# An eight-core trunk kernel: pooling mixer moved into the previous FFN, norm squares summed on GpSimd, first loads reordered

## The chip, the cores and the metric

The kernel runs on one Trainium2 chip, as one program on all eight cores. Each core works on one of the eight sequences of the batch, and the cores do not exchange data. The metric is device time in microseconds (us) of the slowest core, and lower is better.

Engine names are as in the profile: PE is the matrix engine (PEld its weight loads), DVE the vector engine, ACT the scalar engine, POOL GpSimd, SP the engine that issues most DMAs. Cores 0 to 3 form die 0, cores 4 to 7 die 1.

Executions of one kernel fall into two states. In the fast state all cores show nearly the same granted TensorE clock (0.969 to 0.987 of full speed, as a mean over the execution) and times mostly agree within about 0.3%. In the slow state the cores of one die, or of both, show a lower clock and the time is longer. Only fast runs are compared below. A second number is given beside them: the slowest core of each die that was undisturbed (all four clocks at 0.9715 or more), averaged over such dies, even where the other die was slow. It is called "undisturbed dies". It sits a few us under the fast runs, since it takes the slowest of four cores instead of eight, and that core's own span.

## The reference, cut to what matters

```python
D_MODEL = 1024; BATCH = 8; SEQ = 4096; DEPTH = 4; D_FF = 2816
POOL_WINDOWS = (2, 4, 8, 16)      # trailing windows of four channel groups of 256

def reference(x, c, ...):
    c_act = silu(c)
    for i in range(DEPTH):
        mod = c_act @ ada_w[i] + ada_b[i]
        sh1, sc1, g1, sh2, sc2, g2 = split(mod, 6)
        h = rmsnorm(x, norm_mix_g[i]) * (1.0 + sc1) + sh1
        # i % 3: 0 short gated conv, 1 conformer conv, 2 multi-scale pool
        y = mixer(h)
        x = x + g1 * y
        h = rmsnorm(x, norm_ffn_g[i]) * (1.0 + sc2) + sh2
        x = x + g2 * swiglu(h, ffn_w_in[i], ffn_w_out[i])
    return rmsnorm(x, final_g)

def multiscale_pool(h, w_grp, scale):
    # per group g: mean over the last w_g tokens minus the token, then a 256x256 linear
    ...
```

Layers 0 and 3 use the short convolution ("M" below), layer 1 the conformer convolution ("B"), layer 2 the pool ("C"). Every layer ends in a SwiGLU FFN ("F").

## The kernel before

A core holds its sequence channel-major: 8 chunks of 128 channels by the tokens. It goes through the sequence in four blocks of 1024 tokens, s0 to s3. The work of one part of a layer on one block is a *stage* (F1 s3 is the FFN of layer 1 on the last block). A stage is a list of *units*, a unit being one weight slab; each unit is emitted for both halves of the block (`nt` = 0 and 1, 512 tokens each, the width of one projection matmul, 128x512 in the profile). Between the half-units of the current stage the kernel emits small tasks of other work, above all the norm of the next stage; the positions are called *slots* here, and `spread(tasks, lo, hi)` distributes tasks over slots. In the timelines below each engine takes its instructions in the order in which they were emitted (behind the matmuls at 3128.68 us, below, PE stood for 25.45 us before a ones-matmul, with matmuls of the same pool unit emitted behind it).

A norm needs the sum of squares over all 1024 channels, which run along partitions. ACT squares a chunk and PE multiplies it with a matrix of ones, which adds over the partitions and accumulates over the chunks:

```python
def stats_chunk(xk, c, nt):
    bk, bkb = statbank(nt)
    k = sqctr[nt] % 2
    ...
    P.op("act", lambda e: e.activation(sqr2[:, nt, k, :], xres[:, xk, c, tsl(nt)], AF.Square), ...)

    def mm():
        P.op("pe", lambda e: e.matmul(bk, ones_bf[:, :], sqr2[:, nt, k, :], start=(c == 0), stop=(c == 7)), ...)

    pend_stats[nt].append(mm)

def rstd_make(nt):
    flush_stats(nt)                     # emits the pending ones-matmuls
    bk, bkb = statbank(nt)
    rsqrt_eps(rstd_t[:, nt, :], bk, [bkb], [rstdb[nt]])   # two ACT instructions
```

So one norm of a block is 8 chunks times 2 halves, 16 ones-matmuls.

For the pool, the same task that normalises a chunk also forms its window sums on DVE: log2(window) shifted adds (`for l in range(1, g + 2)`), one to four of them:

```python
def norm_pool(xk, c, nt, gs, sh, deps, hk, s):
    tk = norm_chunk(xk, c, nt, gs, deps)          # DVE
    g = c // 2
    w = 2 << g
    H, Hb = scr()
    P.op("act", lambda e: e.activation(H[:, 15:527], tmp_t[:, tk, :], AF.Identity, ...))
    ...                                            # two small DVE copies of 15 columns
    for l in range(1, g + 2):
        ...
        P.op("dve", lambda e: e.tensor_tensor(Sx[:, a:527], prev[:, a:527], prev[:, a - sh_:527 - sh_], ALU.add), ...)
    P.op("dve", lambda e: e.scalar_tensor_tensor(hbuf[...], prev[:, 15:527], 1.0 / w, H[:, 15:527], ALU.mult, ALU.subtract), ...)
```

The pool mixer was the first unit of its own stage "CF"; its norm for the FFN was a second unit without any matmul of its own:

```python
def units_C(st):
    def emit(nt, u):
        slab, slabb = get_slab(u, nt)
        for c in range(8):
            bk, bkb = bank()                       # one of six PSUM banks in rotation
            ...                                    # 2 matmuls
            resid(st, bk, bkb, c, nt, ..., mode="stats")   # DVE: x += ..., then stats_chunk
    unit(st, emit, ("M", 0))

    def emit_norm(nt, u):
        rstd_make(nt)
        for c in range(8):
            norm_h(xk, c, nt, ...)
    unit(st, emit_norm)
...
def ahead(st, part, i, s, frac=None):              # the next stage's norm, inside this stage
    a, b = 2 * st["first"], 2 * st["end"] - 3
    steps = pre_steps(sts[(part, i, s)])
    ...
    spread(steps[:2], t0, t0 + 2)                  # loads
    spread(steps[2:12], t1, t2)                    # squares, ones-matmuls, rstd
    spread(steps[12:], t2, b + 1)                  # norm (and window sums)
```

Weights arrive in f32. The slabs of the first mixer are cast to bf16 by the DMA that loads them, and written back for the later blocks; all other slabs are converted in DRAM beforehand (`conv_tasks`, f32 read and bf16 written), those of the first FFN during stages M0. The slab ring in SBUF has four places. At the start, the ring's loads were issued first:

```python
issue_loads()                                      # four cast loads of weights
st0 = sts[("M", 0, 0)]
pre0 = pre_steps(st0)
pre0[0]()                                          # x of the first half
for t in range(22):
    ada_dma(0, t, ...)                             # conditioning weights
pre0[1]()                                          # x of the second half
...
```

Of the kernel before, what the change touches and what calls it, by code (L numbers as in the profile page):

```python
# [16 lines left out]
F = 2816  # L17
# [243 lines left out]
def build():  # L261
# [14 lines left out]
    with es:  # L276
# [73 lines left out]

        ctr = dict(nb=6, us=0, bank=0, tmp=0, sg=0, scr=0, ub=0)

# [72 lines left out]

        seq = []
        wstate = dict(loaded=0, used=0, done=0)

        def load_slab(g):
# [3 lines left out]
            if s == 0 and (i, p) == (0, "M"):  # L433
                P.op("pool", lambda e: e.dma_start(out=wring[:, k, 0:L], in_=wsrc(i, p, q)), writes=[wb[k]], sem=f"wc{k}", inc=16)
                P.op("sp", lambda e: e.dma_start(out=wdst(i, p, q), in_=wring[:, k, 0:L]), reads=[wb[k]],
                     writes=[wdb[(i, p, q)]], sem=f"wr{k}", inc=16)
            elif s == 0 and name == "bconv":
# [20 lines left out]
        def next_slab():  # L458
            g = wstate["used"]
            assert wstate["loaded"] > g, ("slab not loadable", g, wstate)  # L460
            wstate["used"] += 1
            k = g % NRING
            return wring[:, k, :], wb[k]

# [80 lines left out]
        def rsqrt_eps(out, src, reads, writes):  # L545
            P.op("act", lambda e: e.activation(out, src, AF.Ln, bias=small[:, 16:17], scale=1.0), reads=reads + [constb], writes=writes)  # L546
            P.op("act", lambda e: e.activation(out, out, AF.Exp, bias=small[:, 17:18], scale=-0.5), reads=writes + [constb], writes=writes)  # L547

        def rstd_make(nt):
# [86 lines left out]
        def resid(st, bk, bkb, c, nt, gvec, deps, bias=None, mode="store"):  # L636
# [13 lines left out]
            if mode == "store":  # L650
                x_store(xk, s, nt, c)
            else:
                stats_chunk(xk, c, nt)
# [234 lines left out]
        def units_C(st):  # L888
            i, s, hk, xk = st["i"], st["s"], st["hk"], st["xk"]
# [4 lines that stand above are left out]
                    g, m = c // 2, c % 2  # L894
                    bk, bkb = bank()

                    def fn(pe):
                        for kc in range(2):
                            o = (g * 2 + kc) * 256 + m * 128
                            ins = pe.matmul(bk, slab[:, o:o + 128], hbuf[:, hk, 2 * g + kc, tsl(nt)], start=(kc == 0), stop=(kc == 1))  # L900
                        return ins

                    P.op("pe", fn, reads=[slabb, hb[hk][2 * g][nt], hb[hk][2 * g + 1][nt]], writes=[bkb])
                    resid(st, bk, bkb, c, nt, der[:, i, 16 + c:17 + c], [derb[i][2]], mode="stats")
            unit(st, emit, ("M", 0))

            def emit_norm(nt, u):
                rstd_make(nt)
                for c in range(8):
                    norm_h(xk, c, nt, der[:, i, 8:16], modT[:, i, 24:32], [derb[i][1], modb[i][3]], hk)  # L910
            unit(st, emit_norm)

        def units_F(st, inner=None):
            i, s, hk, xk = st["i"], st["s"], st["hk"], st["xk"]
# [34 lines left out]
            for c in range(8):  # L949
                mk_out(c)  # L950
            if last:
                def emit_out(nt, u):
# [5 lines left out]

        def pre_steps(st):
            part, i, s, xk, hk = st["part"], st["i"], st["s"], st["xk"], st["hk"]  # L960
# [10 lines left out]

            def sq(nt, c):
                flush_stats(nt)
                stats_chunk(xk, c, nt)
                stats_chunk(xk, c + 1, nt)

            def hh(nt, c):
                if part == "CF":
                    norm_pool(xk, c, nt, gs, sh, deps, hk, s)
# [5 lines left out]
            for nt in range(2):  # L985
                for c in range(0, 8, 2):
                    steps.append(lambda nt=nt, c=c: sq(nt, c))
                steps.append(lambda nt=nt: rstd_make(nt))
            for nt in range(2):
# [23 lines left out]

        def ahead(st, part, i, s, frac=None):
            a, b = 2 * st["first"], 2 * st["end"] - 3
            if part is None:
                return
            steps = pre_steps(sts[(part, i, s)])
            if st["part"] == "M":
                t0, t1, t2 = a + 2, a + (b - a) * 3 // 10, a + (b - a) * 6 // 10  # L1020
            else:
                t0, t1, t2 = a + 2, a + 6, a + 22
            if st["part"] == "F" and st["i"] == 3:
                b -= 2
            spread(steps[:2], t0, t0 + 2)
            spread(steps[2:12], t1, t2)
            spread(steps[12:], t2, b + 1)

# [20 lines left out]
        sts[("B3", 1, 3)] = st3  # L1049

        def inner_b3():
            st3["first"] = len(units)
# [3 lines left out]
        for s in range(NPAIR):  # L1056
            stage("F", 1, s, s % 2, lambda st: units_F(st, inner_b3 if s == 0 else None))
        for s in range(NPAIR):
            def cf(st):
                units_C(st)  # L1060
                units_F(st)
            stage("CF", 2, s, s % 2, cf)
        for s in range(NPAIR):
# [7 lines left out]
        for s in range(NPAIR):  # L1071
# [4 lines left out]
            mid = lo + (hi - lo) // 2  # L1076
            spread(steps[2:12], lo - 3, mid)
            spread(steps[12:], mid, hi + 1)
            x3 = pre_steps(sts[("B3", 1, s)])
# [4 lines left out]
            else:  # L1084
# [6 lines left out]
        spread(steps[:2], a, a + 2)  # L1091
        spread(steps[2:12], a + 4, a + 14)
        spread(steps[12:], a + 14, b + 1)
        chain = ([("F", 1, s) for s in range(1, NPAIR)] + [("CF", 2, s) for s in range(NPAIR)]
                 + [("M", 3, s) for s in range(NPAIR)] + [("F", 3, s) for s in range(NPAIR)])
# [8 lines left out]
        for i in range(3):  # L1104
            lo, hi = span("CF" if i == 2 else "F", i, 0, 3)
            spread(ada_tasks(i + 1, range(96)), lo + 4, hi - 12)
# [14 lines left out]
        spread(conv_tasks([(2, "M"), (2, "F")]), lo, hi - 20)  # L1121
        lo, hi = span("CF", 2)
        spread(conv_tasks([(3, "M")]), lo, hi - 20)
        lo, hi = span("M", 3)
        spread(conv_tasks([(3, "F")]), lo - 60, hi - 20)


        issue_loads()
        st0 = sts[("M", 0, 0)]
        pre0 = pre_steps(st0)  # L1130
        pre0[0]()
        for t in range(22):
            ada_dma(0, t, hid2[:, t * 1024:(t + 1) * 1024].bitcast(F32), [hidb[t][0], hidb[t][1]], f"ah{t}", q="sp")
        pre0[1]()
        for fn in pre0[2:12]:
            fn()
        for t in range(22):
            ada_mul(0, t, hid2[:, t * 1024:(t + 1) * 1024].bitcast(F32), [hidb[t][0], hidb[t][1]])
        for fn in ada_tasks(0, range(22, 32)):
            fn()  # L1140
        P.op("dve", lambda e: e.tensor_scalar(der[:, 1, 24:32], vcol("bb1", 8, 8), 0.5, None, ALU.mult), reads=[vecsb], writes=[derb[1][3]])
        P.op("pool", lambda e: e.dma_start(out=wtab[:, :, :, :].rearrange("p a b c -> p (a b c)"), in_=convw_d[:, :]), writes=[wtabb], sem="cvw", inc=16)
# [5 lines left out]
        P.op("sp", lambda e: e.dma_start(out=bones_f[:, :], in_=convc_d[:, 32:160]), writes=[bonesb], sem="cvf", inc=16)  # L1148
        for fn in pre0[12:]:
            fn()  # L1150

# [63 lines left out]
```

## Time and profile before

| | before |
|---|---|
| time, three runs | 5703.26 us median (5702.33 to 6167.07; the last one is slow) |
| profiled core | core 5, 5694.1 us |
| PE busy | 5264.6 us, 92% |
| first projection begins | 93.8 us |
| ones-matmuls | 36 norms x 16 = 576 |
| stretch of the pool layer, F1 s3 to the start of M3 | 1357.0 us |

These are lines of the profile page of the kernel before: the span, the busy time of each engine, and three groups of instructions. A group's columns are source line, engine, operation, output and inputs with their shapes, count, then busy us and mean ns of one, then the engine's idle time just before these instructions and what ended most of it.

```profile
span 5694.1 us, 73906 instructions; the slowest of 8 cores (5674.9 to 5694.1 us)
PE 5264.6 (92%) x24528; PEld 2412.1 (42%) x24528; DVE 2461.0 (43%) x4314; ACT 1620.5 (28%) x2507; POOL 558.4 (10%) x916
...
L627 PE MATMUL psum<-hbuf,wring 128*128 128x512 bf16 x15872 | 3500.6, 381 | 80.1 <-ACT hbuf L563 24.1
...
L540 PE MATMUL psum<-sqr,ones_bf 128*128 128x512 bf16 x576 | 201.6, 400 | 277.4 <-ACT sqr L537 272.1
...
L813 POOL TENSOR_TENSOR hid<-hid 128x512 f32<-128x512 f32 x60 | 99.6, 1660 | 410.0 <-DVE hid L797 409.5
```

PE is busy for 92% of the span, so it is the engine to look at. Its real work is the two projection groups at L627. The ones-matmuls at L540 are 576 of some 24,500 matmuls, yet PE stood idle before them for 277 us: they are where PE waits. POOL does little compute; L813 shows an add of its costing 1.66 us.

Where PE waits is told by windows, which give the busy time of every engine in chosen stretches of time. Columns: start and end of the window, its length, then busy us and count for PE, PEld, DVE, ACT and POOL, the granted clock, the DMA share and GB/s. I take a stage to begin at the first weight load of its projection. The lines are of the kernel before: from the start to the first projection, the four blocks of M0, and the stretch from F1 s3 to the start of M3, which holds all four pool blocks with their FFNs and one plain FFN stage.

```profile
0.00:93.80 93.80, 8.81 (x16) 1.67 (x16) 29.84 (x83) 21.20 (x32) 11.10 (x24) 1.00 0.84 222
93.80:611.10 517.30, 470.70 (x2079) 205.46 (x2080) 352.43 (x713) 130.78 (x214) 77.46 (x144) 0.96 0.79 199
...
2897.10:4254.10 1357.00, 1219.52 (x5553) 544.50 (x5552) 583.90 (x1083) 387.88 (x581) 106.87 (x199) 0.96 0.42 130
```

At full clock one of these matmuls takes 0.2158 us from start to start (1072 matmuls in 231.4 us of a plain FFN stage). The pool stretch has 5552 weight loads, one per matmul, and 5552 x 0.2158 = 1198 us. The PE's waits in the pool layer's stretch of the kernel before (what PE waited for, us in total, times, longest):

```profile
PE psum L540 <- ACT sqr L537: 127.5, 41, 25.5
PE psum L627 <- ACT hbuf L563: 9.7, 4, 2.4
```

The view says "ACT's squares". The timeline of the kernel before, at one of these stops, shows that ACT is only the last link. Columns: start, duration, engine, line, operation; in brackets idle time and what ended it.

```profile
3128.68 1.03 PE L900 MATMUL psum<-hbuf,wring 128*128 128x512 bf16 x4
...
3134.84 0.74 DVE L642 SCALAR_TENSOR_TENSOR xres<-psum,modT,xres 128x512 f32<-128x512 f32 x1
3135.50 0.74 DVE L556 SCALAR_TENSOR_TENSOR tmp<-xres,der,rstd 128x512 f32<-128x512 f32 x1
...
3137.52 2.29 DVE L590 TENSOR_TENSOR aux<-aux 128x518 f32<-128x518 f32 x3
3139.91 0.69 DVE L593 SCALAR_TENSOR_TENSOR hbuf<-aux 128x512 bf16<-128x512 f32 x1
...
3153.55 1.40 DVE L642 SCALAR_TENSOR_TENSOR xres<-psum,der,xres 128x512 f32<-128x512 f32 x2
...
3155.16 0.58 PE L540 MATMUL psum<-sqr,ones_bf 128*128 128x512 bf16 x1 [25.45 <-ACT sqr L537]
```

At 3128.68 PE does the first four matmuls of a pool unit. The ones-matmul emitted behind them needs the square of the first pool residual. That residual (L642 with `der`, at 3153.55) stands on DVE behind window sums of further chunks (L556, L590 with three adds in the lines shown, L593), each of which keeps DVE for 5 to 6 us, and behind residuals of the previous FFN (L642 with `modT`). PE gets to go on at 3155.16, after 25.45 us. DVE works nearly all the while; it only waits some 0.9 us in each chunk for the ACT step of the same window sum.

### The profile page before, as it was taken

What the parts mean: (1) busy time and instruction counts of PE and PEld (TensorE: products, weight loads), DVE (VectorE), ACT (ScalarE), POOL (GpSimd) and SP (SyncE); (2) the same over time, 40 slices, a digit from 0 to 9 for tenths busy, and PEclk for the clock granted to TensorE, in tenths of its full rate; (3) what the DMA queues carried; (4) which work ended last, traced back from release to release, by engine and by line L of the source; (5) the groups of instructions that cost most, each with busy time, mean ns of one, the idle gap of its engine ahead of it and who ended that gap; (6) DMA issues with size and microseconds to landing.
All of it is one profiled execution on the core that took longest, in us unless ns stands there. A gap on an engine that the chain in (4) does not pass through costs nothing.

```text
span 5694.1 us, 73906 instructions; the slowest of 8 cores (5674.9 to 5694.1 us)
## 1 busy us (share of the span) xinstructions
PE 5264.6 (92%) x24528; PEld 2412.1 (42%) x24528; DVE 2461.0 (43%) x4314; ACT 1620.5 (28%) x2507; POOL 558.4 (10%) x916
## 2 busy tenths in 40 slices
PE   3889999999988888999999797979899999999998
PEld 1334444444444444444444343434344444444443
DVE  4667432332285655333224454545326663223222
ACT  2222222122234443222212323232312322323221
POOL 1111110110022111111000010101000000000000
PEclk9999999999998999999999899989999999999999
DMA  7888576854345655666442344435445543233132
GB/s 194 220 212 207 167 177 174 212 146 150 114 168 191 209 204 193 187 191 180 147 153 97 120 137 135 138 132 143 133 130 174 158 138 134 93 112 137 66 111 75
DMA packets 252179, 876.86 MB, mean 154 GB/s; under 512 B 29072, under 2 KB 62096, under 8 KB 220944
## 3 DMA queue, kind: packets, MB, share of 16 engines
q1 hardware_dynamic: 185808, 583.39, 30.9%
q0 software_dynamic: 66000, 288.75, 20.2%
q8 instruction: 205, 3.36, 0.2%
q14 instruction: 166, 1.36, 0.1%
HBM read 813.12 MB, written 219.68 MB: 181 GB/s over the span
## 4 chain that ended last, share of the span: by engine, by line
PE 81%; DVE 7%; DMA 5%; ACT 3%; issue 3%; SPq 0%; DVEq 0%; POOL 0%; ACTq 0%; POOLq 0%
PE psum L627 78%; PE psum L540 2%; DMA xres<-xT 2%; DVE tmp L556 1%; PE psum L790 1%; DMA wring<-wbf 1%; DVE aux L590 1%; DMA wring<-wpack 1%; ACT sqr L537 1%; DMA aux<-adaw 1%; ACT hbuf L563 1%; DVE xres L642 1%; DVE tmp L848 0%; DVE tmp L846 0%; ACT L546 0%
## 5 line engine op out<-in xcount | busy, mean ns | idle before, releaser
L627 PE MATMUL psum<-hbuf,wring 128*128 128x512 bf16 x15872 | 3500.6, 381 | 80.1 <-ACT hbuf L563 24.1
L627 PEld LDWEIGHTS psum<-hbuf,wring 128*128 128x128 bf16 x15872 | 1557.1, 98 | 1977.5 <-issue 138.4
L627 PE MATMUL psum<-hid,wring 128*128 128x512 bf16 x6656 | 1456.3, 379 | 8.4 <-DVE hid L695 8.4
L934 DVE TENSOR_TENSOR hid<-psum,sg 128x512 bf16<-128x512 f32 x704 | 485.1, 691 | 1772.0 <-PE psum L627 1507.3
L627 PEld LDWEIGHTS psum<-hid,wring 128*128 128x128 bf16 x6656 | 650.7, 98 | 794.8 <-issue 12.1
L933 ACT ACTIVATE sg<-psum 128x512 f32<-128x512 f32 x704 | 417.9, 596 | 1506.4 <-PE psum L627 1470.2
L642 DVE SCALAR_TENSOR_TENSOR xres<-psum,modT,xres 128x512 f32<-128x512 f32 x384 | 281.4, 748 | 628.2 <-PE psum L627 624.1
L563 ACT ACTIVATE hbuf<-tmp,modT 128x512 bf16<-128x512 f32 x448 | 313.9, 722 | 800.1 <-DVE tmp L556 799.2
L537 ACT ACTIVATE sqr<-xres 128x512 bf16<-128x512 f32 x576 | 337.3, 622 | 587.5 <-DVE xres L642 332.6
L540 PE MATMUL psum<-sqr,ones_bf 128*128 128x512 bf16 x576 | 201.6, 400 | 277.4 <-ACT sqr L537 272.1
L556 DVE SCALAR_TENSOR_TENSOR tmp<-xres,der,rstd 128x512 f32<-128x512 f32 x512 | 388.9, 788 | 16.3 <-ACT rstd L547 16.3
L618 POOL DMA_DIRECT2D xd<-xres x384 | 209.1, 545 | 1640.4 <-DVE xres L642 876.9
L468 POOL DMA_DIRECT2D aux<-adaw x362 | 195.5, 541 | 1342.3 <-DVE aux L473 1120.2
L473 DVE SCALAR_TENSOR_TENSOR aux<-aux,cbc 128x512 f32<-128x512 f32 x362 | 247.3, 683 | 116.9 <-DMA aux<-adaw 115.0
L540 PEld LDWEIGHTS psum<-sqr,ones_bf 128*128 128x128 bf16 x576 | 57.0, 99 | 392.7 <-issue 348.5
L790 PE MATMUL psum<-aux,wring 128*128 128x256 bf16 x1152 | 160.3, 292 | 37.5 <-DMA wring<-wbf 17.4
L685 ACT ACTIVATE sg<-psum 128x512 f32<-128x512 f32 x128 | 75.6, 591 | 380.0 <-PE psum L627 350.2
L686 DVE TENSOR_TENSOR aux<-psum,sg 128x512 f32<-128x512 f32 x128 | 88.6, 692 | 193.1 <-ACT sg L685 184.5
L790 PEld LDWEIGHTS psum<-aux,wring 128*128 128x128 bf16 x1152 | 118.2, 104 | 70.9 <-issue 43.8
L813 POOL TENSOR_TENSOR hid<-hid 128x512 f32<-128x512 f32 x60 | 99.6, 1660 | 410.0 <-DVE hid L797 409.5
L577 ACT ACTIVATE aux<-tmp,modT 128x512 f32<-128x512 f32 x64 | 46.2, 722 | 301.7 <-DVE tmp L556 301.7
L422 POOL DMA_DIRECT2D wbf<-wpack x93 | 47.6, 512 | 764.1 <-PE psum L627 413.4
(72 smaller groups left out, 1679.0 us busy)
## 6 DMA issues: line engine op xcount, KB each, us to landing
wring<-wbf SPq DMA_DIRECT2D x214, 1024.0 KB, 5.8
xres<-xd SPq DMA_DIRECT2D x112, 1024.0 KB, 11.4
xd<-xres POOLq DMA_DIRECT2D x384, 256.0 KB, 3.6
aux<-adaw POOLq DMA_DIRECT2D x362, 256.0 KB, 5.2
wring<-wbf SPq DMA_DIRECT2D x128, 704.0 KB, 4.3
wbf<-wpack POOLq DMA_DIRECT2D x52, 1024.0 KB, 13.1
wring<-wbf SPq DMA_DIRECT2D x56, 768.0 KB, 6.1
wring<-wbf SPq DMA_DIRECT2D x48, 576.0 KB, 5.5
```

The source lines that it names most:

```text
L468: P.op(q, lambda e: e.dma_start(out=dst, in_=adaw[i, eh]), writes=bufs, sem=sem, inc=16)
L473: P.op("dve", lambda e: e.scalar_tensor_tensor(src, src, 1.0, cbc[:, hf * 512:(hf + 1) * 512], ALU.mult, ALU.mult, accum_out=raw[:, eh:eh ...
L537: P.op("act", lambda e: e.activation(sqr2[:, nt, k, :], xres[:, xk, c, tsl(nt)], AF.Square), reads=[xb[xk][c][nt]], writes=[sq2b[nt][k]])
L540: P.op("pe", lambda e: e.matmul(bk, ones_bf[:, :], sqr2[:, nt, k, :], start=(c == 0), stop=(c == 7)), reads=[sq2b[nt][k], constb], writes= ...
L556: P.op("dve", lambda e: e.scalar_tensor_tensor(tmp_t[:, tk, :], xres[:, xk, c, tsl(nt)], gs[:, c:c + 1], rstd_t[:, nt, :], ALU.mult, ALU.m ...
L563: P.op("act", lambda e: e.activation(hbuf[:, hk, c, tsl(nt)], tmp_t[:, tk, :], AF.Identity, bias=sh[:, c:c + 1], scale=1.0), reads=[tmpb[t ...
L618: P.op("pool", lambda e: e.dma_start(out=xd[s, nt, c], in_=xres[:, xk, c, tsl(nt)]), reads=[xb[xk][c][nt]], writes=[xdb[s][nt][c]], sem=f" ...
L627: ins = pe.matmul(bk, slab[:, k * stride + col0:k * stride + col0 + 128], rhs_fn(k, nt), start=(k == 0), stop=(k == kchunks - 1))
L642: P.op("dve", lambda e: e.scalar_tensor_tensor(xs, bk, gvec, xs, ALU.mult, ALU.add), reads=[bkb] + deps, writes=[xb[xk][c][nt]])
L790: ins = pe.matmul(bk[:, 0:256], slab[:, par * CW + d * 128:par * CW + (d + 1) * 128], uP[:, g, 8 - d:264 - d], start=(d == 0), stop=(d == ...
L933: P.op("act", lambda e: e.activation(sg_t[:, k, :], gt, AF.Silu), reads=[gtb], writes=[sgb[k]])
L934: P.op("dve", lambda e: e.tensor_tensor(hid(hp(f), nt), up, sg_t[:, k, :], ALU.mult), reads=[upb, sgb[k]], writes=[hidb[hp(f)][nt]])
```

## The change

The change has three parts.

1. *Pool mixer in the previous FFN.* The pool unit of block s+1 is placed inside the FFN of block s, behind its third output unit (of block 0, inside F1 s3). Its window sums fall into the slots before; its FFN norm into the slots behind it. The stage "CF" is gone.
2. *Norm squares summed on GpSimd.* ACT squares into f32, POOL adds the eight squares of a half block, and PE does one ones-matmul per half instead of eight. This is done for 23 of the 36 norms, those without it being the norms prepared inside a short-convolution stage, the first one and the final one. It takes 322 matmuls away and puts 322 adds on POOL. With it the slots of the norms move: squares now end two slots earlier, and both halves' rstd are made in one task.
3. *First loads in the order of need.* The conditioning weights and x of the first half are issued first, the four cast loads of weights wait for them (`gate`), and x of the second half is used later. The write-back of the first slabs is issued when a slab is used, not when it is loaded.

```diff
         def load_slab(g):
             if s == 0 and (i, p) == (0, "M"):
-                P.op("pool", lambda e: e.dma_start(out=wring[:, k, 0:L], in_=wsrc(i, p, q)), writes=[wb[k]], sem=f"wc{k}", inc=16)
-                P.op("sp", lambda e: e.dma_start(out=wdst(i, p, q), in_=wring[:, k, 0:L]), ...)
+                P.op("pool", lambda e: e.dma_start(out=wring[:, k, 0:L], in_=wsrc(i, p, q)), writes=[wb[k]],
+                     after=[gate[g]] if g in gate else [], sem=f"wc{k}", inc=16)
...                                      (the write-back moves to next_slab)
+        def sumsq_chunk(xk, c, nt):
+            src = xres[:, xk, c, tsl(nt)]
+            if c == 0:
+                P.op("act", lambda e: e.activation(rstd_t[:, nt, :], src, AF.Square), ...)
+                return
+            k = nxt("sf", 2)
+            ...
+            P.op("act", lambda e: e.activation(sq, src, AF.Square), reads=[xb[xk][c][nt]], writes=sq2b[k])
+            if c < 7:
+                P.op("pool", lambda e: e.tensor_tensor(rstd_t[:, nt, :], rstd_t[:, nt, :], sq, ALU.add), ...)
+                return
+            tot = rstd_t[:, nt, 0:256].bitcast(BF16)
+            P.op("pool", lambda e: e.tensor_tensor(tot, rstd_t[:, nt, :], sq, ALU.add), ...)
+            def mm():
+                P.op("pe", lambda e: e.matmul(bk, ones_bf[:, :], tot, start=True, stop=True), ...)
...
         def units_C(st):
-                    resid(st, bk, bkb, c, nt, ..., mode="stats")
+                    resid(st, bk, bkb, c, nt, ..., mode="keep")
-            def emit_norm(nt, u):  ...
-        def units_F(st, inner=None):
+        def units_F(st, inner=None, late=None):
             for c in range(8):
                 mk_out(c)
+                if c == 2 and late is not None:
+                    late()
...
         def ahead(...):
+            if (part, i) == ("F", 2):
+                c = sts[("C", 2, s)]
+                pool = pre_steps(c)
+                n = 2 * c["first"]
+                spread(pool[:2], a, a + 2)              # loads
+                spread(pool[2:10], a + 3, a + 6)        # squares
+                spread(pool[10:], a + 8, n - 2)         # norm and window sums
+                spread(steps[2:10], n + 1, n + 4)       # squares of the FFN norm
+                spread(steps[10:], n + 6, b + 1)        # FFN norm
+                return
             spread(steps[:2], t0, t0 + 2)
-            spread(steps[2:12], t1, t2)
-            spread(steps[12:], t2, b + 1)
+            spread(steps[2:10], t1, t2 - 2)
+            spread(steps[10:], t2, b + 1)
...
+        for n in range(4):
+            ada_quad(n)                                 # conditioning weights
+        pre0[0]()                                       # x, first half
+        landed = [ada_quad(n) for n in range(4, 8)]
+        gate.update({0: landed[0], 1: landed[2], 2: landed[3], 3: landed[3]})
         issue_loads()
-        pre0[0]()  ...
```

## The prediction

Two passages are cut from the text, where it is marked. No term of its sum is among them: 180 + 30 + 15 + 15 = 240 us stands as it was recorded.

> **What bounds the kernel now.** The TensorE: the page gives PE 92% of 5694 us, the chain of waits puts 78% on projection matmuls. A plain FFN stage runs 231.4 us for 1056 + 16 matmuls (timeline), 0.216 us each, clock 1.00: time is won only by removing matmuls or closing gaps. Gaps (windows, PE waits): 94 us before the first projection; about 45 us in each of four conformer blocks; and the pool layer's stretch, 2965 to 4345 us. Its 5408 projection and pool matmuls need 1167 us, its ones-matmuls 31, yet it takes 1380: 182 us of gaps and of slow matmuls behind them (clock 0.92 to 0.96). The waits name ACT's squares, 127.5 us; the timeline shows why: at 3128.7 PE stops 25.5 us while DVE, in order, works through the next chunks' window sums (4 to 6 us each), the residual behind them; 9 us more for the norm.
>
> **What changes.**
> 1. Pool mixer inside the previous FFN. Its window sums (16 chunks, 55 to 75 us of DVE) fall under FFN-in matmuls, where DVE is 20 to 30% used; squares and norms fall under the last five FFN-out units. The 182 us should go, but the new chain is tight: 14 GpSimd adds plus stores take 20 to 26 us, the ones-matmuls are placed about 24 us after the pool unit, and rstd (4 us) plus eight norms (6.5) reach the next stage about when PE does. I allow 25 us of stall in all. With its share of (2): 209 - 29 = 180 us.
> 2. Ones-matmuls. 23 of 36 norms go from 16 to 2: 322 x 0.216 = 70 us, 27 of them in that stretch. Ten others lie in full FFN stages: 30 us, fully paid. Four in the conformer blocks: 12 us and waits of up to 8 us each for squares, against 14 more adds on GpSimd, busy there already: net 15 us. New: 322 GpSimd adds. Such adds take 1.26 us alone, 1.64 beside a two-input DVE operation, which goes from 0.73 to about 1.2 us. [...] 420 to 530 us busy, mostly hidden.
> 3. Start. SP waits 54.8 us for cast weight loads ahead of x and the conditioning weights. Now about 10 MB are needed first, 45 us at 220 GB/s, then 10 us of DVE: first projection near 60 us. But the second half's x comes late, and deferred loads meet DMAs 0.6 to 0.9 busy; I keep 15 of 34 us.
>
> [...] 0.43 us per matmul after gaps of 8 us.
>
> **Sum.** 180 + 30 + 15 + 15 = 240: 5703 - 240 = 5463 us; 8 in 10: 5415 to 5525. Faster by over 2%: 0.97; within 2%: 0.025; slower: 0.005.
>
> **Right if:** pool-layer stages come every 237 to 245 us (before 271 to 283); ones-matmuls 254 (576); FFN stages 228.4 us; GpSimd near 1000 us; first projection at 55 to 72 us; PE waits of ones-matmuls on GpSimd under 30 us in the pool layer.
>
> **Wrong if:** ACT's squares, their two buffers freed by GpSimd, hold up SiLU and so PSUM; DVE falls behind with window sums, SwiGLU products and conditioning together; GpSimd's backlog stretches the conformer blocks; or the start stays DMA-bound and gives nothing.

## The result, and the profile after

| | before | after |
|---|---|---|
| time, median of four runs | 5705.02 us | 5507.48 us |
| fast runs | 5703.26, 5702.33, 5706.77 | 5497.87, 5503.24, 5511.73 |
| slow runs | 6167.07 | 5736.07 |

All outputs are correct. The ratio after to before is 0.965, with a 95% interval of 0.9628 to 0.9672; a ratio is the mean time of one kernel's fast runs over that of the other's fast runs of the same rounds, so it is not quite the ratio of the medians in the table. The gain is 200 us in the means of the fast runs (5704.1 - 5504.3), against 240 predicted.

The page of the kernel after, the lines that answer to those above:

```profile
span 5496.3 us, 73437 instructions; the slowest of 8 cores (5471.3 to 5496.3 us)
PE 5153.4 (94%) x23750; PEld 2379.6 (43%) x24206; DVE 2480.7 (45%) x4314; ACT 1556.9 (28%) x2469; POOL 986.5 (18%) x1228
...
L652 PE MATMUL psum<-hbuf,wring 128*128 128x512 bf16 x15562 | 3462.5, 381 | 119.3 <-ACT hbuf L588 26.6
...
L563 POOL TENSOR_TENSOR rstd<-rstd,sqr 128x512 f32<-128x512 f32 x276 | 370.9, 1344 | 1236.9 <-ACT sqr L561 1216.9
...
L545 PE MATMUL psum<-sqr,ones_bf 128*128 128x512 bf16 x202 | 72.9, 397 | 89.7 <-ACT sqr L542 86.1
```

The ones-matmuls are down from 576 to 208 + 46 = 254 (L545 shows 202 of the 208: in this trace 1 to 3% of the matmul records are missing, while the weight loads are complete, so I count loads). POOL has gone from 558 to 986.5 us, with adds of 1.344 us in the mean.

Stage starts of the two traces (before: core 5, after: core 2, each the slowest core of a fast run), and the gain of each piece:

| piece | before us | after us | gain |
|---|---|---|---|
| start to first projection | 93.8 | 57.7 | 36.1 |
| M0 | 517.3 | 547.0 | -29.7 |
| F0 | 932.4 | 920.3 | 12.1 |
| conformer, B1 s0 to F1 s0 | 624.6 | 604.6 | 20.0 |
| F1 s0 to s2 | 729.0 | 721.1 | 7.9 |
| pool stretch, F1 s3 to M3 | 1357.0 | 1215.5 | 141.5 |
| M3 | 472.9 | 473.3 | -0.4 |
| F3 | 967.1 | 956.8 | 10.3 |
| whole trace | 5694.1 | 5496.3 | 197.8 |

M0 has become 29.7 us longer and eats most of what the start had won. PE's waits for the squares of the norms prepared there are 25.6 us in the kernel before and 38.0 in the kernel after:

```profile
PE psum L540 <- ACT sqr L537: 25.6, 16, 6.9
...
PE psum L545 <- ACT sqr L542: 38.0, 15, 11.5
```

Experiment e1 comes back to this.

Three of the rows above as the windows of the kernel after give them (columns as before):

```profile
0.00:57.70 57.70, 4.33 (x8) 0.83 (x8) 28.98 (x82) 14.98 (x21) 5.69 (x14) 1.00 0.96 259
57.70:604.70 547.00, 472.50 (x2047) 206.94 (x2089) 353.54 (x713) 137.23 (x224) 78.06 (x144) 0.94 0.82 200
...
2850.70:4066.20 1215.50, 1179.39 (x5319) 532.40 (x5427) 585.96 (x1082) 356.46 (x562) 269.00 (x325) 0.98 0.49 145
```

The pool stretch now has 5427 weight loads, 1171 us at full clock, and takes 1215.5, so 44 us of gaps are left of 159. The 142 us gained are 27 us of ones-matmuls and 115 us of gaps. PE's waits in that stretch of the kernel after:

```profile
PE psum L925 <- DVE xres L667: 26.6, 10, 6.8
PE psum L652 <- DVE hid L953: 3.5, 1, 3.5
```

The waits for squares are gone. What is left is mostly one kind of wait, ten times, 26.6 us. The timeline of the kernel after around the pool unit of the second FFN stage of layer 2:

```profile
3277.61 3.11 DVE L615 TENSOR_TENSOR aux<-aux 128x526 f32<-128x526 f32 x4
3279.97 1.89 PE L925 MATMUL psum<-hbuf,wring 128*128 128x512 bf16 x8
...
3282.05 0.74 DVE L667 SCALAR_TENSOR_TENSOR xres<-psum,modT,xres 128x512 f32<-128x512 f32 x1
...
3282.94 0.59 PE L925 MATMUL psum<-hbuf,wring 128*128 128x512 bf16 x2 [1.07 <-DVE xres L667]
...
3285.01 3.11 DVE L615 TENSOR_TENSOR aux<-aux 128x526 f32<-128x526 f32 x4
...
3289.45 0.75 DVE L667 SCALAR_TENSOR_TENSOR xres<-psum,modT,xres 128x512 f32<-128x512 f32 x1
...
3290.35 1.01 PE L925 MATMUL psum<-hbuf,wring 128*128 128x512 bf16 x2 [6.82 <-DVE xres L667]
...
3290.72 5.36 DVE L667 SCALAR_TENSOR_TENSOR xres<-psum,der,xres 128x512 f32<-128x512 f32 x8
...
3291.62 1.86 PE L925 MATMUL psum<-hbuf,wring 128*128 128x512 bf16 x4 [0.26 <-DVE xres L667]
```

PE begins the pool unit at 3279.97 and runs four chunks (eight matmuls). By the kernel's rotation it then has no free PSUM bank: six banks rotate, and two of them still hold sums of FFN output units whose residual (L667 with `modT`) DVE has not done. DVE is in the last chunks' window sums (L615 x4, 3.11 us of adds, some 7 us per chunk with the norm and the conditioning beside it), and two residuals stand behind two of these chunks. So PE waits 1.07 and 6.82 us. It is the old mechanism in small: work placed in a slot that is shorter than the work, ahead of something that PE needs. An output slot is 4.75 us (22 matmuls x 0.2158).

The second wait in the list, 3.5 us, is POOL's. The timeline of the kernel after, some 35 us into a pool-layer stage:

```profile
3147.23 1.65 POOL L473 DMA_DIRECT2D aux<-adaw  x3
...
3148.89 4.09 POOL L563 TENSOR_TENSOR rstd<-rstd,sqr 128x512 f32<-128x512 f32 x3
...
3153.15 1.79 DVE L478 SCALAR_TENSOR_TENSOR aux<-aux,cbc 128x512 f32<-128x512 f32 x1 [12.15 <-DMA aux<-adaw]
...
3155.70 4.65 PE L652 MATMUL psum<-hbuf,wring 128*128 128x512 bf16 x13 [3.48 <-DVE hid L953]
```

POOL also issues the DMAs of the conditioning weights. Here three issues (L473) come at 3147.23, behind nearly 14 us of adds, and more adds follow; so DVE waits 12.15 us for a conditioning tile, and PE waits 3.48 us for a SwiGLU product (L953) behind it.

### The profile page after: what moved, and what is told of

The parts are those of the page before. It is cut to its first block, busy times and chain, and to the rows that moved or that the text cites. A ratio compares the mean times of both kernels' runs of the same rounds, so it can differ in the third digit from the quotient of the medians.

```text
span 5496.3 us, 73437 instructions; the slowest of 8 cores (5471.3 to 5496.3 us)
## 1 busy us (share of the span) xinstructions
PE 5153.4 (94%) x23750; PEld 2379.6 (43%) x24206; DVE 2480.7 (45%) x4314; ACT 1556.9 (28%) x2469; POOL 986.5 (18%) x1228
## 4 chain that ended last, share of the span: by engine, by line
PE 80%; DVE 6%; DMA 6%; issue 3%; ACT 2%; POOL 1%; SPq 1%; DVEq 0%; ACTq 0%; POOLq 0%
PE psum L652 78%; DMA aux<-adaw 2%; DMA xres<-xT 2%; DMA wring<-wbf 1%; PE psum L815 1%; DVE tmp L581 1%; POOL rstd L563 1%; DVE tmp L873 1%; DVE aux L615 1%; PE psum L545 1%; DVE tmp L871 1%; DVE xres L667 0%; ACT sqr L542 0%; DVE hid L783 0%; PE psum L925 0%
## 5 line engine op out<-in xcount | busy, mean ns | idle before, releaser
L652 PE MATMUL psum<-hbuf,wring 128*128 128x512 bf16 x15562 | 3462.5, 381 | 119.3 <-ACT hbuf L588 26.6
L953 DVE TENSOR_TENSOR hid<-psum,sg 128x512 bf16<-128x512 f32 x704 | 483.9, 691 | 1525.1 <-PE psum L652 1118.2
L667 DVE SCALAR_TENSOR_TENSOR xres<-psum,modT,xres 128x512 f32<-128x512 f32 x384 | 281.8, 749 | 699.5 <-PE psum L652 689.9
L563 POOL TENSOR_TENSOR rstd<-rstd,sqr 128x512 f32<-128x512 f32 x276 | 370.9, 1344 | 1236.9 <-ACT sqr L561 1216.9
L473 POOL DMA_DIRECT2D aux<-adaw x352 | 191.7, 545 | 790.9 <-DVE aux L478 473.5
L478 DVE SCALAR_TENSOR_TENSOR aux<-aux,cbc 128x512 f32<-128x512 f32 x352 | 260.2, 739 | 153.7 <-DMA aux<-adaw 153.2
L561 ACT ACTIVATE sqr<-xres 128x512 f32<-128x512 f32 x322 | 193.2, 624 | 168.2 <-POOL rstd L563 156.3
L542 ACT ACTIVATE sqr<-xres 128x512 bf16<-128x512 f32 x208 | 122.4, 624 | 324.5 <-DVE xres L667 254.9
L545 PE MATMUL psum<-sqr,ones_bf 128*128 128x512 bf16 x202 | 72.9, 397 | 89.7 <-ACT sqr L542 86.1
L615 DVE TENSOR_TENSOR aux<-aux 128x512 f32<-128x512 f32 (+6 forms) x160 | 111.1, 694 | 10.4 <-DVE aux L615 0.5
```

Source lines behind the costliest of these rows:

```text
L473: P.op(q, lambda e: e.dma_start(out=dst, in_=adaw[i, eh]), writes=bufs, sem=sem, inc=16)
L478: P.op("dve", lambda e: e.scalar_tensor_tensor(src, src, 1.0, cbc[:, hf * 512:(hf + 1) * 512], ALU.mult, ALU.mult, accum_out=raw[:, eh:eh ...
L561: P.op("act", lambda e: e.activation(sq, src, AF.Square), reads=[xb[xk][c][nt]], writes=sq2b[k])
L563: P.op("pool", lambda e: e.tensor_tensor(rstd_t[:, nt, :], rstd_t[:, nt, :], sq, ALU.add), reads=sq2b[k], writes=[rstdb[nt]])
L652: ins = pe.matmul(bk, slab[:, k * stride + col0:k * stride + col0 + 128], rhs_fn(k, nt), start=(k == 0), stop=(k == kchunks - 1))
L667: P.op("dve", lambda e: e.scalar_tensor_tensor(xs, bk, gvec, xs, ALU.mult, ALU.add), reads=[bkb] + deps, writes=[xb[xk][c][nt]])
```

## The experiments

Three experiments take the change apart (e1 to e3), five each work on one remaining wait or try one more step (e4 to e7, e11), and three combine (e8 to e10). They ran in three batches, each with its own runs of the kernel before: fast means 5700.2 us (batch one, e1 to e4), 5707.8 (batch two, e5 to e8), 5699.6 (batch three, e9 to e11); undisturbed dies 5695.0, 5702.9 and 5695.6. The kernel after has 5498.4 us on undisturbed dies. All kernels gave correct results. The kernel before itself moved by up to 8 us between batches, so a difference of that size to the kernel after is not resolved.

My theory was that the three parts act through three separate stretches of time and nearly add up, that the remaining stall at the pool unit is the order of DVE's window sums, and that the lead at the start is lost because stages M0 are limited by DMA. The rivals are named with each experiment.

### e1: only the load order

The kernel before with part 3 alone:

```diff
+        gate = {}
...
+                     after=[gate[g]] if g in gate else [], sem=f"wc{k}", inc=16)
...
+        for n in range(4):
+            ada_quad(n)
+        pre0[0]()
+        landed = [ada_quad(n) for n in range(4, 8)]
         issue_loads()
```

> The kernel before with only the new order of first loads. Theory A (the layer-0 mixer is bound by DMA bytes, 124 MB up to the first FFN stage in both traces, at about 205 GB/s): the first projection comes near 58 us instead of 94, the lead shrinks from stage to stage and is 5 to 10 us at the first FFN stage; the whole kernel is 5 to 10 us faster, ratio 0.998 to 0.999. Rival B (the lead is lost once, because x of the second half lands late and PE waits at about 62 to 82 us): the lead is already down to 10 us when the second mixer stage starts and stays there. If neither holds and the start pays in full: 30 us or more faster.

Of eight executions only one was fast: 5683.07 us, 17 us under the kernel before (0.997). Seven undisturbed dies give 5678.3, 16.7 us under. The profiled run was slow on die 0:

```profile
die 0 (median of its cores): 6171.1 us, clock 0.878
die 1 (median of its cores): 5672.5 us, clock 0.973
```

so only die 1 can be read. There (core 4, against core 5 of before) the first projection leads by 34.0 us, the blocks of M0 by 29.9, 22.8 and 26.6, and F0 begins 24.6 us early. The rival, that the lead is down to 10 us after the first block, falls: 30 of the 34 us are still there at the second block. But theory A, a lead that shrinks to 5 to 10 us at F0, is missed as well: 24.6 us are left.

Why then is the lead at F0 only 6.4 us between the kernel before and the kernel after? Start of F0 and PE's waits for squares during M0, as means over the cores of each trace (of its undisturbed die for e1 and e2; worked out from the starts and waits of every core):

| start | slots of the norms in M0 | runs | F0 begins, us | waits for squares in M0, us |
|---|---|---|---|---|
| old | old | before | 609.0 | 26 |
| new | old | e1 | 586.4 | 15 |
| old | shifted | e2, e3 | 627.0, 622.8 | 44, 49 |
| new | shifted | after, e4, e6, e7, e11 | 601.3, 594.1, 598.9, 598.9, 595.8 | 33 to 39 |

Kernels with the same slots show a lead of 23 us (e1 against before) or 27 (the means of the two last rows). Kernels with the same start begin F0 some 16 (old start) or 11 us (new start) later with the shifted slots, and PE waits 18 to 24 us longer for squares. So the shifted slots, a by-product of part 2, probably take back in M0 about half of what part 3 wins there. It is not shown by a run of its own: no experiment changed these slots alone, and each kernel has one traced execution.

### e2: only the pool mixer moved

The kernel after with the old start and the old sums (the shifted slots stay):

```diff
         def pre_steps(st, slim=True):
+            slim = False
```

(and the hunks of part 3 taken back).

> The kernel before with only the pool mixer moved into the previous FFN stage; the norms keep their 16 ones-matmuls each. Theory: the pool layer's stretch loses 141 us in the full change, of which the fewer ones-matmuls there are 27 us, so this part alone gives 105 to 125 us, ratio 0.978 to 0.982, with the same stalls of PE at the pool unit (7 to 8 us a stage, behind DVE). Rival: GpSimd's sums were what kept the new chain short, and PE now waits for ACT's squares after the pool unit; then under 90 us.

One fast run, 5625.73 us, 74 us under the kernel before (0.987); five undisturbed dies at 5621.6, 73 under. That is the rival's size. The pool stretch alone gains 80 us; before F0 the trace loses 16. The waits of PE in the pool stretch of e2 (core 7, on its undisturbed die):

```profile
PE psum L921 <- DVE xres L663: 26.4, 9, 6.6
PE psum L541 <- ACT sqr L538: 23.4, 24, 1.7
```

The first line is the stall at the pool unit, the same as in the kernel after. The second is new: now the norm's squares are pressed into few slots behind the pool unit, and the ones-matmuls wait for ACT 24 times. From one pool unit to the next e2 takes 259 to 263 us, the kernel after 246 to 248.

### e3: only the sums on GpSimd

The kernel before with `sumsq_chunk` and its slots:

```diff
             def sq(nt, c):
+                if slim:
+                    sumsq_chunk(xk, c, nt)
+                    sumsq_chunk(xk, c + 1, nt)
+                    return
...
-                t0, t1, t2 = a + 2, a + 6, a + 22
+                t0, t1, t2 = a + 2, a + 6, a + 19
```

Without the moved pool mixer 19 norms can use it, 266 matmuls. The shift of the slots came with it and moves the old window sums too, so this run does not isolate the sums in the pool stretch.

> The kernel before with only the GpSimd sums of squares (19 of 36 norms go from 16 ones-matmuls to 2; the pool layer stays as it was). Theory: 19 x 14 = 266 matmuls x 0.216 us = 57 us, plus up to 10 us in the conformer blocks where PE waited for squares: 55 to 70 us, ratio 0.988 to 0.990. Rival: the adds cost as much as they save wherever DVE is busy [...]: under 40 us, with the loss in the conformer blocks and in the pool layer.

One fast run, 5629.73 us, 70 us under (0.988); six undisturbed dies at 5625.3. By pieces: F0 12.1, conformer 20.9, F1 7.6, pool stretch 34, F3 12.5. Against that, 16.8 us are lost before F0 (the shifted slots again, see e1) and 4.2 in M3. In F0, the conformer, F1 and F3 these are the gains of the whole change, to a microsecond or two, so the FFN and conformer gains belong to the sums. The 34 us in the pool stretch are more than the 15 us that its 70 fewer matmuls are worth; how much of that is the shifted slots, this run cannot say.

Together: 17 + 74 + 70 = 161 us for the parts, 200 for the whole, some 39 more. In the pool stretch (means over cores) the parts give 110 us and the whole 144, and two terms of these 34 us are visible. The four norms between pool and FFN only become cheap with both parts, 4 x 14 = 56 matmuls x 0.2158 = 12 us; and e2's 23.4 us of waits for squares are absent in the kernel after. That makes 35. Before F0 the parts lose 9 us together and the whole gains 8, 17 more, because e2 and e3 both have the shifted slots and the whole has them once. In the conformer the whole gains 6.5 us less than the parts together. The rest is within what single fast runs can tell.

### e4: dear chunks first

The kernel after, with the window sums in chunk order 7 to 0, so that the chunks with four adds come early, under the FFN's input units, and the cheap ones just before the pool unit:

```diff
-                for c in range(8):
+                for c in (range(7, -1, -1) if part == "C" else range(8)):
                     steps.append(lambda nt=nt, c=c: hh(nt, c))
```

> The changed kernel with the pool's window sums of each half done in the order of chunks 7 to 0 instead of 0 to 7: same instructions, same slots, but the chunks with four adds no longer come last. Theory (PE stops 7 to 8 us at each pool unit because DVE, in order, still has the longest window sums ahead of the residuals that free PSUM): the stops fall under 3 us a stage, 20 to 30 us in all, ratio to before 0.960 to 0.962. Rival (eight residuals need more than the six PSUM banks, whatever is ahead of them): no change, 0.965.

Fast runs 5472.46 and 5472.65, ratio to the kernel before 0.9601 (0.9578 to 0.9624); seven undisturbed dies at 5469.7, 29 us under the kernel after. The pool stretch is 1196.0 us, 19.5 under. The same wait at the pool unit in e4's pool stretch:

```profile
PE psum L925 <- DVE xres L667: 12.6, 6, 4.3
```

26.6 us have become 12.6. The order of the window sums is thus a cause of the stall, and about half of it; the rival (too few PSUM banks, whatever stands ahead) expected no change. About 9 us of the gain came in M0, which the edit does not touch; the five kernels with this M0 begin F0 between 594.1 and 601.3 us (table in e1), so I take it as chance.

### e5: eight slabs of the first FFN cast on load

The kernel after, but the eight output slabs of the first FFN are not converted in DRAM during M0; the DMA that loads them for block 0 casts them and they are written back from SBUF, as for the first mixer. That takes reads and writes out of M0.

```diff
-            if s == 0 and (i, p) == (0, "M"):
+            if s == 0 and ((i, p) == (0, "M") or ((i, p) == (0, "F") and q >= 11)):
...
-        spread(conv_tasks([(0, "F")]), lo + 14, hi - 8)
+        spread(conv_tasks([(0, "F")])[:11], lo + 14, hi - 8)
```

> The changed kernel, but the eight output slabs of the first FFN are cast when the first FFN stage loads them instead of being converted in DRAM during the layer-0 mixer: 17 MB of 124 MB leave the layer-0 mixer. Theory (that mixer is bound by DMA bytes at about 205 GB/s, which is why part of the 33 us won at the start is given back): the first FFN stage starts 20 to 50 us earlier than in the changed kernel (600 us), part of it lost again while the first FFN stage loads more; 10 to 35 us in all, ratio to before 0.959 to 0.963. Rival (the lead is lost by waits that have nothing to do with bytes): within 8 us of 600, ratio 0.965.

Fast runs 5488.64 and 5491.23, ratio 0.9618 (0.9595 to 0.9642); five undisturbed dies at 5485.8, 12.6 us under the kernel after. F0 begins at 579.5 us instead of 604.7, and the profile counts 118.30 MB moved until then instead of 124.08, at the same rate (204 and 205 GB/s). So M0 is limited at least in part by what DMA has to do; bytes and the number of DMA issues on POOL were not separated, as both leave M0 together. That the lead at the start is lost to it does not follow: e1 keeps most of its lead with all bytes in place. Where my expectations speak of 17 MB of 124, two counts are mixed: the profile counts a casting DMA at its bf16 size (704 KB for each of these slabs, 5.8 MB for the eight), while by their shapes 11.5 MB of f32 are read and 5.8 MB of bf16 written.

But the first stage of F0 gives most of it back. The window and the PE's longest kind of wait there in e5:

```profile
579.50:828.00 248.50, 233.15 (x1069) 104.86 (x1068) 78.34 (x145) 53.36 (x84) 54.71 (x81) 0.97 0.75 190
```

```profile
PE psum L652 <- DMA wring<-wpack: 15.3, 3, 12.2
```

against the same stage of the kernel after:

```profile
604.70:835.20 230.50, 229.34 (x1047) 104.50 (x1068) 77.32 (x144) 53.33 (x84) 51.52 (x74) 1.00 0.69 181
```

The e5 window takes 248.5 instead of 230.5 us, mostly because PE waits 15.3 us for the cast loads (`wpack` is the f32 source); the longest of these waits is 12.2 us. Before F0 in e5, a cast load of 768 KB took 11.9 us from issue to landing in the median, a plain load of that size 9.6. (Both windows reach 2.1 us into the next stage; the stage itself takes 246.4 and 228.4 us.)

### e6: GpSimd sums in layer 3's mixer too

```diff
-            steps = pre_steps(sts[(part, i, s)], st["part"] != "M")
+            steps = pre_steps(sts[(part, i, s)], st["part"] != "M" or st["i"] == 3)
```

> The changed kernel with the GpSimd sums also where the layer-3 mixer prepares the next stage (four more norms, 56 fewer ones-matmuls). Theory (GpSimd's adds are hidden wherever PE is the bound): 56 x 0.216 = 12 us faster, ratio 0.963, layer-3 mixer stages 115.7 us apart instead of 118.7. Rival (the mixer's DVE, 65% busy with two-input operations, slows [...], and the sums are late for the ones-matmul): no gain or a loss, ratio 0.965 or more, with PE waiting for GpSimd.

Fast runs 5488.49 and 5523.11, ratio 0.9646 (0.9594 to 0.9699), which cannot be told from the kernel after; six undisturbed dies at 5485.9, 12.5 us under it. In the traces the piece from M3 to F3 gains 7 us, where 12 were expected, and PE's waits for DVE's `hid` products grow there from 1.3 to 16.0 us (core 5 of e6). It is a small gain and I do not claim its size.

### e7: window sums earlier

The kernel after, with the window sums of the pool in slots two earlier at the beginning and three earlier at the end:

```diff
-                spread(pool[10:], a + 8, n - 2)
+                spread(pool[10:], a + 6, n - 5)
```

> The changed kernel with the pool's window sums spread from two slots earlier and ending three slots earlier, same work and same order. Theory (PE stops at the pool unit because DVE is behind with window sums): the stop of 6.8 us goes at least by two thirds, 20 to 35 us in all, ratio 0.959 to 0.962. Rival (DVE is used so fully by then that starting earlier only moves the stop into the FFN-in units): under 10 us, new waits of PE for DVE's SwiGLU products.

One fast run, 5482.47 us (0.9605 to the kernel before); five undisturbed dies at 5478.0, 20 us under the kernel after. The pool stretch is 1195.7 us, 19.8 under. The wait at the pool unit in e7's pool stretch:

```profile
PE psum L925 <- DVE xres L667: 13.1, 3, 5.6
```

It is halved, as in e4, by an edit that leaves the order alone and only moves the work out of the last output slots. The longest stop falls from 6.8 to 5.6 us, less than the two thirds that I expected. Both edits have one thing in common: less of DVE's work stands ahead of the residuals at the pool unit.

### e8: everything together

e4, e5, e6 and e7 in one kernel.

> Four edits together on the changed kernel: heavy window sums first, window sums earlier, GpSimd sums in the layer-3 mixer, and the first FFN's output slabs cast on load. Theory: they act at different places, so most adds up: 45 to 80 us against the changed kernel, ratio to before 0.951 to 0.957, 5425 to 5460 us. Rival: the two edits of the window sums cure the same stop, and the rest is noise: 0.959 to 0.961.

Fast runs 5439.87 and 5441.28, ratio 0.9532 (0.9509 to 0.9555); seven undisturbed dies at 5438.6. The pool stretch is 1175.7 us, where the bare matmuls take 1171. PE's largest wait in it:

```profile
PE psum L652 <- DVE hid L953: 2.1, 1, 2.1
```

No wait at the pool unit (L925) is left. The two edits of the window sums, 19.5 and 19.8 us alone, add up to 40: each alone left half of the wait, both together none of it. The other two edits in e8 do not act there: e5 and e6 alone leave the stretch at 1214.1 and 1215.4 us. The six PSUM banks are the same in all of these, so too few banks, the rival in e4, is not the cause.

### e9: the eight slabs converted later

To keep e5's lead without its stall: the eight slabs are again converted in DRAM, not during M0 but in the first half of F0's first stage, before they are needed there; the conversions for layer 1 come behind them.

```diff
-        spread(conv_tasks([(0, "F")]), lo + 14, hi - 8)
+        spread(conv_tasks([(0, "F")])[:11], lo + 14, hi - 8)
         lo, hi = span("F", 0)
-        spread(conv_tasks([(1, "B1"), (1, "B3"), (1, "F")]), lo, hi - 10)
+        spread(conv_tasks([(0, "F")])[11:], lo - 2, lo + 18)
+        spread(conv_tasks([(1, "B1"), (1, "B3"), (1, "F")]), lo + 22, hi - 10)
```

(with e4, e6 and e7).

> As the four edits together, but the first FFN's eight output slabs are still converted in DRAM, only later: in the first FFN stage's first half, with the conversions for layer 1 moved behind them. Theory (cast on load made that stage 18 us longer because each load waited for a ring slot and then for f32 bytes; conversion ahead of the load does not hold the ring): the first FFN stage keeps the 25 us lead, 10 to 18 us faster than the four edits with the cast (5440 us), ratio 0.950 to 0.952. Rival (that stage is then bound by bytes as well): 5435 to 5450 us, the stage again near 250 us long.

Fast runs 5420.61 and 5410.92, mean 5415.8, a ratio of 0.950 to the kernel before; six undisturbed dies at 5415.2. It is the fastest kernel: 284 us under the kernel before of its own rounds, where the kernel after is 200 us under that of its rounds; on undisturbed dies it is 83 us under the kernel after. The first stage of F0 and the pool stretch in e9:

```profile
572.60:803.10 230.50, 229.34 (x1047) 104.44 (x1068) 76.61 (x143) 53.33 (x84) 53.54 (x78) 1.00 0.69 183
```

```profile
2817.90:3998.00 1180.10, 1168.69 (x5319) 530.28 (x5427) 584.50 (x1082) 355.49 (x562) 268.56 (x325) 1.00 0.50 150
```

F0's first stage is back at 230.5 us and has kept the lead of 32 us over the kernel after. The same bytes cost PE nothing here, where the DMA share is 0.69 in both kernels, while in M0 it is 0.77 to 0.82 (windows of e9 and of the kernel after).

### e10: only four slabs cast on load

e8 with four slabs instead of eight (`q >= 15`, `[:15]`).

> As the four edits together, but only the last four output slabs are cast on load. Theory (bytes only move between two stages, and the first FFN stage has room for about half of them): lead at the first FFN stage 10 to 15 us, of which under 6 are given back; 5432 to 5442 us. Rival (any cast on load stalls the ring by its own latency): as much given back per slab as with eight, 5440 to 5450 us.

No execution was fast. Undisturbed dies gave 5468, 5444, 5462 and 5439 us, too few and too far apart. The run is inconclusive.

### e11: the adds on DVE instead of GpSimd

The kernel after, with the 322 adds of the squares on the vector engine:

```diff
-                P.op("pool", lambda e: e.tensor_tensor(rstd_t[:, nt, :], rstd_t[:, nt, :], sq, ALU.add), ...)
+                P.op("dve", lambda e: e.tensor_tensor(rstd_t[:, nt, :], rstd_t[:, nt, :], sq, ALU.add), ...)
```

> The changed kernel with the 322 adds of squares on VectorE instead of GpSimd. Theory (what pays is the 322 ones-matmuls gone; the engine of the adds matters only where DVE is full): plain FFN stages unchanged at 228.4 us, the pool layer's stages and the conformer blocks slower, 10 to 40 us slower in all, ratio 0.967 to 0.972. Rival ([...] GpSimd's adds cost DVE as much as its own 0.69 us): within 8 us of the changed kernel, 0.964 to 0.966.

Fast runs 5502.96, 5514.08 and 5532.81, ratio 0.968 (0.9637 to 0.9722) to the kernel before; six undisturbed dies at 5500.7, 2 us from the kernel after. (The fast runs' mean is 12 us above that of the kernel after; the two slower of the three have die 1 at a clock of 0.969 to 0.977, so I go by the undisturbed dies.) The busy line of e11's page:

```profile
PE 5165.9 (94%) x23750; PEld 2383.3 (43%) x24206; DVE 2654.9 (48%) x4636; ACT 1556.7 (28%) x2469; POOL 556.1 (10%) x906
```

430 us have gone from POOL, 174 have come to DVE (276 of the adds are one line of the page, L563: 1344 ns each in the mean on POOL, 688 on DVE). From the start of F0 on, the trace of e11 is 12 us slower than that of the kernel after, 8.5 of it in the conformer. So the choice of GpSimd is worth at most about 12 us. What pays is that 322 matmuls and their waits are gone, not which engine adds.

What the adds on POOL and DVE's work cost each other can be read in the kernel after, in one place where the two overlap in time:

```profile
3318.10 4.35 POOL L563 TENSOR_TENSOR rstd<-rstd,sqr 128x512 f32<-128x512 f32 x3
...
3318.56 1.35 DVE L478 SCALAR_TENSOR_TENSOR aux<-aux,cbc 128x512 f32<-128x512 f32 x1
```

Three adds beside DVE's conditioning product take 4.35 us, 1.45 each, where one alone takes 1.27; and the product (L478) takes 1.35 us, where alone it takes 0.68. With the adds on DVE (e11) the 352 products of L478 take 685 ns in the mean, in the kernel after 739. Why both are longer together the traces do not show; they give durations only.

## Why the prediction was right or wrong

The total is inside the range, 5507 us in 5415 to 5525, and the direction is right, but it lies 44 us on the slow side of the estimate. By the four terms of the sum:

- **Ones-matmuls in full FFN stages, 30 us: right.** F0, F1 and F3 gain 12.1 + 7.9 + 10.3 = 30.3 us in the traces, and e3 confirms that the sums alone do it. FFN stages now take 228.4 us, as said, and the ones-matmuls are 254, as said.
- **Conformer blocks, 15 us: right, slightly low.** 20.0 us in the traces, 20.9 in e3. This excess makes up for part of the shortfall at the start, which is luck.
- **Start, 15 us of 34: the size right for the start alone, the reason not.** The first projection begins at 57.7 us (55 to 72 were said). By itself the new start is worth 17 us (e1), with a lead of 23 to 27 us at F0 among kernels with the same slots. The reason that I named, late x and deferred loads on a busy DMA, explains at most the loss from 34 to 25 us in e1. In the whole change only 6.4 us are left at F0. The sum had no term for what part 2 costs in M0: its shifted slots raise PE's waits for squares there (25.6 to 38.0 us in the traces) and delay F0 by 11 to 16 us in the means (e1). That cause is likely, not isolated.
- **Pool stretch, 180 us: the term that was mis-sized; 141.5 us.** Two things went into it. The first is my reading of the profile of before: "2965 to 4345 us" begins 68 us inside stage F1 s3 and ends 91 us inside M3, so it is 23 us longer than the stretch whose matmuls I set against it. With the stage starts counted off, "1380", "182" and "209" become 1357, 159 and 186. The second is the stall allowed: 44 us of gaps are left, not 25. The wait at the pool unit is 26.6 us of them, the wait behind POOL's queue 3.5; the rest, about 14 us, I put down to matmuls at a lower clock after these stops, which fits the granted clock of 0.98 but was not measured by itself. Together: 23 us too much expected, and 44 instead of the 29 that the sum took off, 15 us: 38 us, which is 180 - 141.5.

The mechanism named for the pool stretch was right: windows and waits show that the waits for squares are gone. From one pool unit to the next the time is 248.2, 247.4 and 245.7 us (289.1, 280.4 and 282.3 before), just outside the 237 to 245 predicted. What I named as the tight place was not the tight place. I expected the chain behind the pool unit (adds, ones-matmuls, rstd, norm) to arrive late; PE's waits on POOL for ones-matmuls are 1.6 us in all. The stall sits before it, in the window sums that I thought hidden under the FFN-in matmuls: most are, but the last chunks, which are the dearest, fall into 4.75 us output slots. "DVE falls behind with window sums" stood in the list of what would make the prediction wrong, and e4, e7 and e8 show that it is the cause: two edits of DVE's order and room take the pool stretch to within 5 us of its bare matmuls.

The slow matmuls that the prediction saw ("0.43 us per matmul after gaps of 8 us") (granted clock 0.50 from 1910.7 to 1914 us of the kernel before) are there in the kernel after too. The two matmuls behind the 6.82 us stop take 1.01 us and the next four 1.86 us (both shown above), 0.46 to 0.5 each, against 0.2158 at full clock; the granted clock was 0.50 from 3290 to 3294 us.

The remaining surprise is that the parts do not add: 161 us apart, 200 together (e1 to e3). The moved pool mixer alone presses its norm into few slots and pays 23.4 us for squares; with the sums that wait is gone.

What stays open: whether M0 gains the 11 to 16 us when its norms go back to the old slots (a run with only `spread` for stages M restored would tell); how much of e3's pool gain is the shifted slots; and what the better number of slabs to cast on load is (e10). The seven to twelve us of e6 are not settled either.

## What to carry to other kernels

Look at what stands in an engine's queue ahead of the instruction that frees another engine's buffer: a wait in PE's list named "ACT squares" (127.5 us before) or "DVE residual" (26.6 us after) was, in the pool stretch, long work of the same DVE placed too late, and moving it (dear items first, and a few free slots before the point of need) closed it (none left at the pool unit in e8). Take a stretch that you cost from stage boundaries that are counted off in the instruction order, not by eye, or the gain that you expect contains someone else's time. When an edit shifts the slots of a helper, check every stage that uses it: here a shift made for the FFN stages probably cost time in M0. Here it was better to move the conversion of eight slabs from M0 (DMA share 0.77 to 0.82) to F0's first stage, which stayed at 230.5 us with a share of 0.69 (e9), than to cast them in the loads that PE needs, which made that stage 248.5 us (e5).
